# Seven block products in place of eight for 20 of the 32 hidden tiles of the down product

## The chip, the cores and the metric

One core of one Trainium2 chip runs the whole step. The metric is the device time in microseconds; three runs of the kernel before gave 1573.73, 1575.43 and 1575.45, median 1575.43.

## The reference, cut to what matters

One decoder layer for 1024 prompt rows and 8 sample rows (T = 1032 columns; the kernel keeps everything transposed, channels on the 128 partitions). The change touches the second half, with D = 1024 and D_FF = 4096, all in float32:

```python
    x = layer_norm(ALPHA * x + (1 + g1) * m, ln1_g, ln1_b)
    v = x * (1 + sc2) + sh2
    hid = jnp.square(jax.nn.relu(jnp.einsum('bld,df->blf', v, w_up)))
    x = layer_norm(ALPHA * x + (1 + g2) * jnp.einsum('blf,fd->bld', hid, w_down), ln2_g, ln2_b)
```

The gate g2 is one vector for the prompt rows and one for each sample row.

## The kernel before

Every large product is done in three matmuls for one (`term`, L204): a float32 operand is split into a high part (a copy rounded to the faster format fp32r, on ScalarE) and a low part (the rest, a subtraction on VectorE; `split`, L201), and high*high, low*high and high*low are summed in PSUM. `product` (L212) runs, for each of three blocks of 344 columns, all these matmuls into one PSUM bank and then calls an evacuation. A matmul instruction carries a weight load of 128 columns of its own.

The second half has 32 hidden tiles of 128 channels. `hidden(i)` (L949) makes one: 72 matmuls of 344 columns (8 input tiles, 3 terms, 3 blocks), then for each block a relu on ScalarE (from PSUM), a square on VectorE, a rounded copy on ScalarE and a subtraction on VectorE (L944, L945). The down product adds the hidden tiles, times `w_down` and the gate, to the eight residual tiles `x1[m]`, which lie in SBUF in the slabs U0 to U7: `gate_add` (L786) reads a PSUM block on VectorE, multiplies by the gate, adds to `x1[m]` (L789), and treats the 8 sample columns with two small operations (L792, L793).

The tiles are taken in chunks: five of 4 (L985) and two of 6 (L1002). In a chunk of 4, after the four `hidden` come four pairs of output tiles `mp`; each pair takes 2 output tiles, 3 blocks, 4 hidden tiles and 3 terms, which is 72 matmuls of 344 columns, and 6 `gate_add`. In the last chunk the residual is first shifted by a rounded mean (`row_shift`, L994, with the subtractions at L1010) and the second layer norm runs between the last products, over the column blocks of 392, 384 and 256 columns of `LAST`.

Weights come through `weights` (L193), which takes the oldest of two prepared sets and starts on another: a DMA on SP's queue into one of two `raw` buffers (L146), then `parts` splits it into `whi` and `wlo`, two buffers each, so the set after next is split once the set before the next one is used up. The list `order` (L156 to L175) fixes the sequence. PSUM has four banks for `product` (tag mm), one for `ada` and three for `sm`. The order of instructions on each engine is chosen when the kernel is built, by a planner that runs through a time line of its own and, of the instructions that are ready in it, takes the one that stands first in the program; each engine then works through its queue in that fixed order.

Of the kernel before, what the change touches and what calls it, by code (L numbers as in the profile page):

```python
# [17 lines left out]
P = 128  # L18
D = 1024
TP = 1024  # L20
# [34 lines left out]
NFB = 2  # L55
NFA = (DFF // P - 6 * NFB) // 4

# [7 lines left out]
def cols(ap, b):  # L65
    return ap[:, b[0]:b[1]]


def build(tc, ctx, a):
# [10 lines left out]
    pm = ctx.enter_context(tc.tile_pool(name="pm", bufs=MMB, space=PSUM))  # L80
    pq = ctx.enter_context(tc.tile_pool(name="pq", bufs=7 - MMB, space=PSUM))
    dp = ctx.enter_context(tc.tile_pool(name="dp", bufs=1, space=DRAM))

    uid = [0]

    def nm(s):
        uid[0] += 1
        return f"{s}_{uid[0]}"
# [4 lines left out]
    def tmp(w=T, dt=F32):  # L93
        return sp.tile([P, w], dt, tag="t", name=nm("t"), bufs=5)

    def psm():
        return pm.tile([P, 512], F32, tag="mm", name=nm("mm"))
# [69 lines left out]
    for f in range(NFA):  # L167
        order += [("wup", i) + ((("raw", "aw", "yt"),) if i == 2 else ()) for i in range(4 * f, 4 * f + 4)]
        order += [("wda", f, mp) for mp in range(4)]
    spare = [f"U{i}" for i in range(8, 14)] + ["C0", "C1", "C2", "C3", "G", "G"]  # L170
    for f in range(NFB):
        order += [("wup", 4 * NFA + 6 * f + i) for i in range(6)]
        for m in range(8):
            tags = ("raw", spare[2 * m - 4], spare[2 * m - 3])
            order.append(("wdb", f, m) + ((tags,) if f == NFB - 1 and m > 1 else ()))  # L175
# [12 lines left out]
    def prefetch():  # L188
        if order:
            key, raw = load_next()  # L190
            ahead.append((key, parts(*raw)))
# [802 lines left out]
    def row_shift():  # L994

        near, base = tmp(dt=F32R), tmp()
        nc.scalar.copy(near, x1[0])
        for b in BLOCKS:
            ln1.total(base, (cols(near, b),), P, b, w=rones)
        return base  # L1000

    for f in range(NFB):  # L1002
        if f == NFB - 1:
            base = row_shift()
        kh = []
        for i in range(6):
            kh.append(hidden(4 * NFA + 6 * f + i))
            if f == NFB - 1:
                for m in ((0, 1), (2, 3, 4), (5, 6, 7), (), (), ())[i]:
                    tc.keep_in_program_order(tt(x1[m], x1[m], base, op=ALU.subtract))  # L1010
        kf = [(i, h, l) for i, (h, l) in enumerate(kh)]
        if f < NFB - 1:
            for m in range(8):
                product(weights("wdb", f, m), kf, lambda b, ps: gate_add(x1[m], ps, M_G2, m, b))
            continue
# [56 lines left out]
        for m in range(8):  # L1072
            wd.append(weights("wdb", f, m))
            down(m, b)
            if m:
                add_x(m, b)
                add_q(m, b)
# [129 lines left out]
```

## Time and profile before

| | us |
|---|---|
| median of 3 runs | 1575.43 |
| profiled execution, its own time | 1574.45 |
| its span (first to last instruction) | 1572.6 |
| TensorE busy | 1541.8 (98%) |
| VectorE busy | 868.6 (55%) |
| ScalarE busy | 526.3 (33%) |
| mean granted TensorE clock | 0.994 |

A profiled execution is read first by the share of each engine, then by the chain of work that ended last, then by stretches. A matmul's duration in the trace (320 ns at 344 columns) is longer than the distance between two of them, since they overlap; what a matmul costs in a dense stretch is the stretch divided by the count.

### The profile page before, as it was taken

Reading aid. Unit: us, or ns where it says so; the run is one execution under the profiler, and the core shown is the slowest. Engines: PE = TensorE matmul, PEld = TensorE weight load, DVE = VectorE, ACT = ScalarE, POOL = GpSimd, SP = SyncE. Lnnn points to the kernel's source line nnn. Section 1 sums busy time; section 2 is a strip of 40 time slices with the busy share of each in tenths; the row PEclk is TensorE's granted clock in tenths of the full one; section 3 lists DMA queues with packets and bytes.
Section 4 is the critical chain, followed back from the end, with each engine's and each line's share of the span. In section 5 each row is a group of like instructions: output and inputs, shape, how many; then the busy total and the mean of one; then the engine's idle time right before and its main releaser. Section 6 shows DMA issues by size and latency. Waiting matters only on the chain.

```text
span 1572.6 us, 23959 instructions
## 1 busy us (share of the span) xinstructions
PE 1541.8 (98%) x10058; PEld 1489.2 (95%) x10058; DVE 868.6 (55%) x1653; ACT 526.3 (33%) x805; POOL 169.0 (11%) x168
## 2 busy tenths in 40 slices
PE   6999999999999999999999999999999999999996
PEld 5899999999889999999999999999999999999995
DVE  4575556677876742636996444434343433335477
ACT  2553323323333353613577121121312213113334
POOL 0004222221211311100241000000000000000001
PEclk9999999999999999999999999999999999999998
DMA  9332344344343323412221111111111111111102
GB/s 366 114 118 94 108 132 141 118 140 132 135 151 128 119 96 108 175 42 93 82 68 54 41 54 41 48 47 42 53 41 54 41 54 34 45 56 51 61 31 88
DMA packets 49628, 141.44 MB, mean 90 GB/s; under 512 B 5736, under 2 KB 14696, under 8 KB 49520
## 3 DMA queue, kind: packets, MB, share of 16 engines
q1 hardware_dynamic: 49520, 139.91, 27.4%
q8 instruction: 79, 1.29, 0.3%
q14 instruction: 29, 0.24, 0.1%
HBM read 126.33 MB, written 13.56 MB: 89 GB/s over the span
## 4 chain that ended last, share of the span: by engine, by line
PE 94%; DVE 3%; DMA 1%; ACT 1%; issue 1%; POOL 0%; SPq 0%; ACTq 0%; DVEq 0%; POOLq 0%
PE mm L210 86%; PE ada L229 2%; PE sm L651 1%; PE sm L643 1%; PE sm L842 1%; PE sm L638 1%; PE sm L673 1%; PE sm L210 1%; DMA S<-in_xT 0%; PE sm L617 0%; DVE U L1055 0%; PE sm L236 0%; DMA s<-in_ssm 0%; PE sm L597 0%; PE mm L425 0%
## 5 line engine op out<-in xcount | busy, mean ns | idle before, releaser
L210 PE MATMUL mm<-U,whi 128*128 128x344 f32 x3058 | 778.5, 323 | 4.6 <-ACT U L336 4.6
L210 PEld LDWEIGHTS mm<-U,whi 128*128 128x128 f32 x3058 | 536.6, 188 | 21.4 <-issue 11.8
L210 PE MATMUL mm<-U,wlo 128*128 128x344 f32 x1529 | 488.1, 322 | 0.0
L202 ACT CAST whi<-raw 128x1024 fp32r<-128x1024 f32 (+1 forms) x122 | 125.7, 1030 | 544.0 <-PE mm L210 529.8
L210 PEld LDWEIGHTS mm<-U,wlo 128*128 128x128 f32 x1529 | 286.9, 188 | 3.0 <-issue 2.8
L789 DVE SCALAR_TENSOR_TENSOR U<-mm,mod,U 128x344 f32<-128x344 f32 (+3 forms) x216 | 122.7, 571 | 206.5 <-PE mm L210 206.5
L210 PE MATMUL mm<-S,whi 128*128 128x344 f32 (+3 forms) x912 | 232.8, 320 | 0.0
L202 DVE TENSOR_TENSOR wlo<-raw,whi 128x1024 fp32r<-128x1024 f32 (+1 forms) x122 | 146.5, 1201 | 132.2 <-ACT whi L202 131.8
L210 PEld LDWEIGHTS mm<-S,whi 128*128 128x128 f32 x912 | 160.6, 188 | 0.3
L210 PE MATMUL mm<-S,wlo 128*128 128x344 f32 (+3 forms) x456 | 145.3, 320 | 0.0
L210 PE MATMUL mm<-C,whi 128*128 128x344 f32 x516 | 143.0, 320 | 0.0
L944 DVE TENSOR_TENSOR t<-t 128x344 f32<-128x344 f32 x96 | 49.3, 515 | 87.5 <-ACT t L944 87.5
L210 PEld LDWEIGHTS mm<-C,whi 128*128 128x128 f32 x516 | 92.9, 188 | 0.1
L210 PEld LDWEIGHTS mm<-S,wlo 128*128 128x128 f32 x456 | 85.6, 188 | 0.1
L1057 POOL TENSOR_SCALAR U<-U,vec 128x392 f32<-128x392 f32 (+1 forms) x4 | 5.6, 1388 | 720.0 <-DVE U L1055 720.0
L210 PE MATMUL mm<-C,wlo 128*128 128x344 f32 x258 | 82.5, 320 | 0.0
L210 PE MATMUL mm<-G,whi 128*128 128x344 f32 x258 | 82.1, 321 | 0.1
L210 PE MATMUL mm<-xg,whi 128*128 128x344 f32 x258 | 82.0, 320 | 0.0
L387 DVE SCALAR_TENSOR_TENSOR t<-t,vec,t 128x1064 f32<-128x1064 f32 (+1 forms) x52 | 71.8, 1388 | 10.7 <-ACT t L385 9.7
L944 ACT ACTIVATE t<-mm 128x344 f32<-128x344 f32 x96 | 43.6, 455 | 97.0 <-PE mm L210 97.0
L210 PE MATMUL mm<-yc,whi 128*128 128x344 f32 x210 | 66.8, 322 | 0.0
L945 DVE TENSOR_TENSOR S<-t,S 128x344 fp32r<-128x344 f32 x66 | 33.9, 516 | 29.6 <-ACT S L944 29.3
(360 smaller groups left out, 2117.7 us busy)
## 6 DMA issues: line engine op xcount, KB each, us to landing
raw<-in_win SPq DMA_DIRECT2D x44, 512.0 KB, 3.7
aw<-in_wada SPq DMA_DIRECT2D x33, 512.0 KB, 4.2
raw<-in_wup SPq DMA_DIRECT2D x32, 512.0 KB, 3.5
raw<-in_wout SPq DMA_DIRECT2D x24, 512.0 KB, 3.5
raw<-in_wda SPq DMA_DIRECT2D x20, 512.0 KB, 3.5
G<-acd SPq DMA_DIRECT2D x16, 512.0 KB, 3.9
raw<-in_wdb SPq DMA_DIRECT2D x16, 384.0 KB, 3.1
S<-in_xT SPq DMA_DIRECT2D x8, 516.0 KB, 10.2
```

Of the source, the lines that this page charges most:

```text
L202: return nc.scalar.copy(thi, src), tt(tlo, src, thi, op=ALU.subtract)
L210: mm(ps[:, :b[1] - b[0]], wt, cols(xt, b), start=(i == 0 and q == 0), stop=(i == n - 1 and q == 2))
L229: mm(ps[32 * g:32 * g + 32, :256], cs[:, 2 * kp + k2, :], w[:, c:c + 256], start=(kp == 0), stop=(kp == KD // 2 - 1), tile_position=(0, 32 ...
L387: stt(r, t[:, k:k + n], wt(k), r, op0=ALU.mult, op1=ALU.add)
L638: mm(po[:, i * P:(i + 1) * P], st[:, h0:h0 + P], bc[2 + g][:, sl], start=True, stop=True)
L643: mm(py[r * HD:(r + 1) * HD, i * P:(i + 1) * P], xg[g][:, 0, h * HD:(h + 1) * HD], Gs[g][:, h, :], start=True, stop=True, tile_position=(0 ...
L651: mm(pst, bt[:, g * P:(g + 1) * P], xg[g][:, 1], start=True, stop=True)
L673: mm(pn[:, :BW], w, cols(src, b), start=(i == 0), stop=(i == len(srcs) - 1))
L789: stt(dst[:, lo:hi], ps[:, :hi - lo], mod[:, row + m, 0:1], dst[:, lo:hi], op0=ALU.mult, op1=ALU.add)
L842: mm(pn, w, src, start=(i == 0), stop=(i == len(srcs) - 1))
L944: return [lambda: act(x, ps, AF.Relu), lambda: tt(x, x, x, op=ALU.mult), lambda: nc.scalar.copy(xh, x), lambda: tt(xl, x, xh, op=ALU.subtr ...
L945: lambda: tt(xl, x, xh, op=ALU.subtract)]
```

## The change

Hidden tiles 0 to 5 and 26 to 31 keep the plain product, in chunks of 6 at the beginning and the end. The 20 tiles between them form five groups of 4, and in a group each pair of output tiles is done as a 2x2 block product: the 4 hidden tiles are two halves of 2, the 2 output tiles are two halves, and the 1032 columns are two halves of 516. A half of the columns is two runs of 258 (`four`: the first and third quarter, or the second and fourth). Seven products of sums take the place of eight (Winograd's form): `seven` runs them, 12 matmuls of 258 columns each (2 runs, 2 hidden tiles, 3 terms), each into a pair of PSUM banks. Some products are added on top of what a pair holds after it was read; so a pair is read by VectorE (`add_rows`, 516 columns, one operation) and then written on by a later product: `u` takes products 1, 3, 5 and 7, `v` 2 and 6, `y` 4. Seven `add_rows` replace six `gate_add`; the sample columns of three of them are summed in `acc8` and gated at the end.

The operand sums of the hidden tiles (`operands`) and of the weights (`seven_parts`) are made on VectorE and split like the other operands. The split of the four weight sums goes into one single pair of buffers, U2 and U3: for `mp` 0 at once, for 1 and 2 after the `seven` before, and for 3 piece by piece, each sum after the product of `mp` 2 that last reads its place. `hidden_raw` leaves the hidden tile unsplit. Three of the next group's up products stand between the down products (after `operands(0)`, after `mp` 0 and after `mp` 1), the fourth at the head of the next group; `mp` 2 and 3 follow each other directly. U0 and U1 take hidden sums too, and the residual goes to DRAM (`x1d`): each `seven` loads the two rows of the next pair and stores its own two. The PSUM tiles stay single banks as far as the first chunk; `pairs` then closes these pools and opens three pairs for the products and two banks for `sm`. The host lays `w_down` out to suit.

```diff
-NFB = 2
-NFA = (DFF // P - 6 * NFB) // 4
+NFS = 5
+NF = 6
+SPAIR = 0, 2, 1, 3
+QW = T // 4
...
+    stack = ctx.enter_context(ExitStack())
+    pm = stack.enter_context(tc.tile_pool(name="pm", bufs=MMB, space=PSUM))
+    pq = stack.enter_context(tc.tile_pool(name="pq", bufs=7 - MMB, space=PSUM))
...
+    large = []
+    turn = [0]
     def psm():
-        return pm.tile([P, 512], F32, tag="mm", name=nm("mm"))
+        if not large:
+            return pm.tile([P, 512], F32, tag="mm", name=nm("mm"))
+        i = turn[0] % 6
+        turn[0] += 1
+        return large[i % 3][:, i // 3]
+    def pairs():
+        nonlocal pq
+        stack.close()
+        pf = ctx.enter_context(tc.tile_pool(name="pf", bufs=1, space=PSUM))
+        large.extend(pf.tile([P, 2, 512], F32, tag=f"mm{i}", name=f"mm{i}") for i in range(3))
+        pq = ctx.enter_context(tc.tile_pool(name="pg", bufs=2, space=PSUM))
...
-    for f in range(NFA):
-        order += [("wup", i) + ((("raw", "aw", "yt"),) if i == 2 else ()) for i in range(4 * f, 4 * f + 4)]
-        order += [("wda", f, mp) for mp in range(4)]
+    def up(i):
+        return [("wup", i) + ((("raw", "aw", "yt"),) if i == 2 else ())]
+    for i in range(NF):
+        order += up(i)
+    order += [("wdb", 0, m) for m in range(8)]
+    for f in range(NFS):
+        n = NF + 4 * f
+        order += (up(n) if f == 0 else []) + [x for i in SPAIR[f > 0 and 3 or 1:] for x in up(n + i)]
+        nxt = [n + 4 + i for i in (SPAIR if f < NFS - 1 else range(4))]
+        order += up(nxt[0])
+        for mp in range(4):
+            order.append(("wds", f, mp))
+            if mp < 2:
+                order += up(nxt[1 + mp])
+    for i in range(3, NF):
+        order += up(NF + 4 * NFS + i)
     spare = [f"U{i}" for i in range(8, 14)] + ["C0", "C1", "C2", "C3", "G", "G"]
...
+    for m in range(8):
+        tags = ("raw", spare[2 * m - 4], spare[2 * m - 3])
+        order.append(("wdb", 1, m) + ((tags,) if m > 1 else ()))
...
-            ahead.append((key, parts(*raw)))
+            ahead.append((key, parts(*raw) if key[0] != "wds" else seven_parts(raw[0], key[2])))
+    sums2 = []
+    later = []
+    def seven_parts(raw, mp):
+        ha, la = part("whi", F32R, 768), part("wlo", F32R, 768)
+        if not sums2:
+            sums2.extend((part("U2", F32R, 1024), part("U3", F32R, 1024)))
+        hb, lb = sums2
+        a11, a12, a22, a21 = (raw[:, 256 * i:256 * i + 256] for i in range(4))
+        (s1, s2), (s3, s4) = ([t[:, :256], t[:, 256:]] for t in (part("wb", F32, 512), part("wc", F32, 512)))
+        tt(s3, a11, a21, op=ALU.subtract)
+        tt(s1, a21, a22, op=ALU.add)
+        tt(s2, s1, a11, op=ALU.subtract)
+        tt(s4, a12, s2, op=ALU.subtract)
+        got = {}
+        def pieces(src, h, l, *names):
+            w = 256 * len(names)
+            split(src, h[:, :w], l[:, :w])
+            for i, k in enumerate(names):
+                got[k] = h[:, 256 * i:256 * i + 256], l[:, 256 * i:256 * i + 256]
+        pieces(raw[:, :256], ha, la, "a11")
+        pieces(raw[:, 256:768], ha[:, 256:], la[:, 256:], "a12", "a22")
+        def sum_pieces(*names):
+            for k in names:
+                i, src = {"s3": (0, s3), "s2": (1, s2), "s1": (2, s1), "s4": (3, s4)}[k]
+                pieces(src, hb[:, 256 * i:256 * i + 256], lb[:, 256 * i:256 * i + 256], k)
+        if mp:
+            later.append(sum_pieces)
+        else:
+            sum_pieces("s3", "s2", "s1", "s4")
+        return got
...
-    for f in range(NFA):
-        kh = [t[2] for t in two] if f == 0 else []
-        kh += [hidden(4 * f + i) for i in range(len(kh), 4)]
+    eight = cp.tile([P, 8, NS], F32, tag="ysm", name="eight")
+    x1d = [dp.tile([P, T], F32, tag=f"x1d{m}", name=f"x1d{m}") for m in range(8)]
+    kh = [t[2] for t in two] + [hidden(i) for i in range(2, NF)]
+    kf = [(i, h, l) for i, (h, l) in enumerate(kh)]
+    for m in range(8):
+        product(weights("wdb", 0, m), kf, lambda b, ps: gate_add(x1[m], ps, M_G2, m, b))
+        nc.gpsimd.tensor_copy(eight[:, m], x1[m][:, TP:])
+        dma(x1d[m], x1[m])
+    def four(t):
+        return t.rearrange("p (a h c) -> p a h c", a=2, h=2)
+    def hidden_raw(i):
+        r = tmp()
+        product(weights("wup", i), kv, lambda b, ps: act(cols(r, b), ps, AF.Relu))
+        tt(r, r, r, op=ALU.mult)
+        return r
+    sops = {}
+    def operands(j, ra, rb):
+        if j == 0:
+            sops["b11"] = pair(("S0", "S1"))
+        tags = {"b2": (("S2", "S3"), ("U14", "U15")), "odd": (("S4", "S5"), ("yt", "st")), "even": (("S6", "S7"), ("U0", "U1"))}
+        hl = {k: pair(t[j]) for k, t in tags.items()}
+        for k, names in (("b2", ("b21", "b22")), ("odd", ("t1", "t3")), ("even", ("t2", "t4"))):
+            for h, name in enumerate(names):
+                sops[name, j] = [four(t)[:, :, h] for t in hl[k]]
+        for p in range(2):
+            a_, b_ = four(ra)[:, p], four(rb)[:, p]
+            c = (2 * j + p) * QW
+            split(a_[:, 0], *(x[:, c:c + QW] for x in sops["b11"]))
+            t = tmp()
+            t1, t3, t2, t4 = (t[:, i * QW:(i + 1) * QW] for i in range(4))
+            tt(t1, a_[:, 1], a_[:, 0], op=ALU.subtract)
+            tt(t3, b_[:, 1], a_[:, 1], op=ALU.subtract)
+            tt(t2, b_[:, 1], t1, op=ALU.subtract)
+            tt(t4, b_[:, 0], t2, op=ALU.subtract)
+            w = slice(2 * QW * p, 2 * QW * p + 2 * QW)
+            split(rb[:, w], *(x[:, w] for x in hl["b2"]))
+            split(t[:, :2 * QW], *(x[:, w] for x in hl["odd"]))
+            split(t[:, 2 * QW:], *(x[:, w] for x in hl["even"]))
+    acc8 = cp.tile([P, 8, NS], F32, tag="xsm", name="acc8")
+    nc.vector.memset(acc8, 0.0)
+    def add_rows(ps, row, m, h):
+        d = four(row)[:, :, h]
+        if h:
+            tt(acc8[:, m], acc8[:, m], ps[:, 1, QW - NS:QW], op=ALU.add)
+        stt(d, ps[:, :, :QW], mod[:, M_G2 + m, 0:1], d, op0=ALU.mult, op1=ALU.add)
+    def load_rows(mp):
+        rows = [slab(f"U{4 + m % 4}") for m in (2 * mp, 2 * mp + 1)]
+        for i, r in enumerate(rows):
+            dma(r, x1d[2 * mp + i])
+        return rows
+    def seven(f, mp):
+        w = weights("wds", f, mp)
+        m1, m2 = 2 * mp, 2 * mp + 1
+        (r1, r2), last = rows[0], f == NFS - 1
+        if mp < 3 or not last:
+            rows[0] = load_rows((mp + 1) % 4)
+        def multiply(ps, a_, b_, first=False):
+            for p in range(2):
+                for j in range(2):
+                    wh, wl = (t[:, j * P:(j + 1) * P] for t in w[a_])
+                    if b_ == "b11":
+                        xh, xl = (t[:, (2 * j + p) * QW:(2 * j + p + 1) * QW] for t in sops["b11"])
+                    else:
+                        xh, xl = (t[:, p] for t in sops[b_, j])
+                    for q, (wt, xt) in enumerate(((wh, xh), (wl, xh), (wh, xl))):
+                        mm(ps[:, p, :QW], wt, xt, start=first and j == 0 and q == 0, stop=(j == 1 and q == 2),
+                           skip_group_check=not first)
+            if mp == 2 and a_[0] == "s":
+                later[0](a_)
+        u, y, v = (large[(turn[0] + i) % 3] for i in range(3))
+        multiply(u, "a11", "b11", True)
+        add_rows(u, r1, m1, 0)
+        multiply(v, "s3", "t3", True)
+        add_rows(v, r2, m2, 1)
+        multiply(u, "s2", "t2")
+        add_rows(u, r2, m2, 0)
+        multiply(y, "a12", "b21", True)
+        add_rows(y, r1, m1, 0)
+        multiply(u, "s1", "t1")
+        add_rows(u, r2, m2, 1)
+        multiply(v, "a22", "t4")
+        add_rows(v, r2, m2, 0)
+        multiply(u, "s4", "b22")
+        add_rows(u, r1, m1, 1)
+        if last and mp > 1:
+            x1[m1], x1[m2] = r1, r2
+        else:
+            for m, r in ((m1, r1), (m2, r2)):
+                dma(x1d[m], r)
+    pairs()
+    rows = [load_rows(0)]
+    r = [hidden_raw(NF + i) for i in SPAIR]
+    for f in range(NFS):
+        n = NF + 4 * f
+        nxt = [n + 4 + i for i in (SPAIR if f < NFS - 1 else range(4))]
+        if f:
+            r.append(hidden_raw(n + SPAIR[3]))
+        operands(0, r[0], r[1])
+        more = [hidden_raw(nxt[0])]
+        operands(1, r[2], r[3])
         for mp in range(4):
-            w = weights("wda", f, mp)
-            for m in (2 * mp, 2 * mp + 1):
-                product(w, [(4 * (m % 2) + i, h, l) for i, (h, l) in enumerate(kh)],
-                        lambda b, ps: gate_add(x1[m], ps, M_G2, m, b))
...
+            seven(f, mp)
+            if mp < 3:
+                done = later.pop(0)
+                if mp < 2:
+                    done("s3", "s2", "s1", "s4")
+            turn[0] += 1
+            if mp < 2:
+                more.append(hidden_raw(nxt[1 + mp]))
+        r = more
+    kh = []
+    for x in r:
+        h, l = pair(ht[hn % len(ht)])
+        hn += 1
+        split(x, h, l)
+        kh.append((h, l))
+    for m in range(4):
+        x1[m] = slab(f"U{m}")
+        dma(x1[m], x1d[m])
+    tt(acc8, acc8, mod[:, M_G2:M_G2 + 8, 1:9], op=ALU.mult)
+    tt(acc8, acc8, eight, op=ALU.add)
+    for m in range(8):
+        nc.gpsimd.tensor_copy(x1[m][:, TP:], acc8[:, m])
+    for i in range(3, NF):
+        kh.append(hidden(NF + 4 * NFS + i))
+        if i == 3:
+            near, base = tmp(dt=F32R), tmp()
+            nc.scalar.copy(near, x1[0])
+            for b in BLOCKS:
+                ln1.total(base, (cols(near, b),), P, b, w=rones)
+        for m in ((0, 1, 2, 3), (4, 5, 6, 7), ())[i - 3]:
+            tc.keep_in_program_order(tt(x1[m], x1[m], base, op=ALU.subtract))
+    kf = [(i, h, l) for i, (h, l) in enumerate(kh)]
+    if ks:
         total = ln1.total
...
```

## Rows read from the trace of the kernel before

**Rows 1.** Page, part 1 (busy time, share, instructions) and part 4 (chain by engine).
```profile
PE 1541.8 (98%) x10058; PEld 1489.2 (95%) x10058; DVE 868.6 (55%) x1653; ACT 526.3 (33%) x805; POOL 169.0 (11%) x168
...
PE 94%; DVE 3%; DMA 1%; ACT 1%; issue 1%; POOL 0%; SPq 0%; ACTq 0%; DVEq 0%; POOLq 0%
```

**Rows 2.** Chain of waits in order of time, from 842 us: start, length, what.
```profile
842.18 572.69 PE mm L210 x3630
...
1415.34 99.09 PE mm L210 x606
```

**Rows 3.** Stretches: busy time and count by engine, clock, DMA share, GB/s.
```profile
842.18:1414.55 572.37, 572.37 (x3630) 572.37 (x3630) 231.34 (x449) 129.37 (x220) 0.00 (x0) 1.00 0.15 47
1483.31:1508.84 25.53, 25.53 (x146) 25.53 (x144) 19.02 (x42) 9.48 (x15) 0.00 (x0) 1.00 0.24 78
1535.58:1540.10 4.52, 4.52 (x40) 4.52 (x39) 4.32 (x9) 1.37 (x3) 0.33 (x1) 1.00 0.12 44
```

**Rows 4.** VectorE groups by shape, from 842 us: busy us, mean ns | idle.
```profile
L202 DVE TENSOR_TENSOR wlo<-raw,whi 128x1024 fp32r<-128x1024 f32 x49 | 60.0, 1225 | 77.0 <-ACT whi L202 77.0
L789 DVE SCALAR_TENSOR_TENSOR U<-mm,mod,U 128x344 f32<-128x344 f32 x96 | 55.2, 575 | 93.4 <-PE mm L210 93.4
L944 DVE TENSOR_TENSOR t<-t 128x344 f32<-128x344 f32 x95 | 48.8, 515 | 86.8 <-ACT t L944 86.8
...
L789 DVE SCALAR_TENSOR_TENSOR U<-mm,mod,U 128x384 f32<-128x384 f32 x16 | 9.8, 614 | 6.4 <-PE mm L210 6.4
...
L1010 DVE TENSOR_TENSOR U<-U,t 128x1032 f32<-128x1032 f32 x8 | 9.4, 1227 | 0.0
...
L792 DVE TENSOR_TENSOR gs<-mm,mod 128x8 f32<-128x8 f32 x56 | 8.7, 156 | 0.0
...
L789 DVE SCALAR_TENSOR_TENSOR U<-mm,mod,U 128x256 f32<-128x256 f32 x8 | 3.8, 479 | 0.0
...
L1040 DVE TENSOR_TENSOR xg<-yc,xg 128x256 f32<-128x256 f32 x1 | 0.4, 425 | 0.8 <-ACT yc L846 0.8
```

**Rows 5.** Timeline of VectorE, 874 to 885 us: start, length, what [idle].
```profile
877.34 1.05 DVE L789 SCALAR_TENSOR_TENSOR U<-mm,mod,U 128x344 f32<-128x344 f32 x2 [3.06 <-PE mm L210]
...
882.39 1.22 DVE L202 TENSOR_TENSOR wlo<-raw,whi 128x1024 fp32r<-128x1024 f32 x1 [0.28 <-ACT whi L202]
883.54 0.57 DVE L789 SCALAR_TENSOR_TENSOR U<-mm,mod,U 128x344 f32<-128x344 f32 x1
```

**Rows 6.** ScalarE groups by shape, the same stretch and columns.
```profile
L202 ACT CAST whi<-raw 128x1024 fp32r<-128x1024 f32 x49 | 51.4, 1049 | 267.6 <-PE mm L210 267.6
L944 ACT ACTIVATE t<-mm 128x344 f32<-128x344 f32 x94 | 42.7, 455 | 97.0 <-PE mm L210 97.0
L944 ACT CAST S<-t 128x344 fp32r<-128x344 f32 x64 | 30.6, 481 | 50.5 <-DVE t L944 50.5
```

**Rows 7.** Timeline of all engines at a block's end, 879 us.
```profile
879.03 0.47 PE L210 MATMUL mm<-S,whi 128*128 128x344 f32 x2
...
879.38 0.58 DVE L789 SCALAR_TENSOR_TENSOR U<-mm,mod,U 128x344 f32<-128x344 f32 x1 [0.72 <-PE mm L210]
```

**Rows 8.** Timeline of all engines, 734 to 736 us: TensorE waits for VectorE.
```profile
734.11 1.22 DVE L202 TENSOR_TENSOR S<-raw,S 128x1024 fp32r<-128x1024 f32 x1
...
734.50 0.32 PE L210 MATMUL mm<-U,whi 128*128 128x344 f32 x1
...
735.38 0.59 PE L210 MATMUL mm<-yc,S 128*128 128x344 f32 x2 [0.56 <-DVE S L202]
```

**Rows 9.** DMA issues of the whole run: count, KB each, us to landing.
```profile
raw<-in_wda SPq DMA_DIRECT2D x20, 512.0 KB, 3.5
...
ycd<-yc SPq DMA_DIRECT2D x8, 516.0 KB, 3.1
t<-ycd SPq DMA_DIRECT2D x8, 516.0 KB, 4.6
U<-in_xT SPq DMA_DIRECT2D x8, 516.0 KB, 7.9
```

More of the change, by code (lines that the diff above doesn't have):

```diff
@@ L79, in build @@
     sp = ctx.enter_context(tc.tile_pool(name="sp", bufs=1))
-    pm = ctx.enter_context(tc.tile_pool(name="pm", bufs=MMB, space=PSUM))
-    pq = ctx.enter_context(tc.tile_pool(name="pq", bufs=7 - MMB, space=PSUM))
     dp = ctx.enter_context(tc.tile_pool(name="dp", bufs=1, space=DRAM))
+    stack = ctx.enter_context(ExitStack())
+    pm = stack.enter_context(tc.tile_pool(name="pm", bufs=MMB, space=PSUM))
+    pq = stack.enter_context(tc.tile_pool(name="pq", bufs=7 - MMB, space=PSUM))
     uid = [0]
@@ L166, in build @@
             order.append(("wout", 1, m) + ((("raw", f"S{m}", f"S{m + 1}"),) if m % 2 == 0 else ()))
-    for f in range(NFA):
-        order += [("wup", i) + ((("raw", "aw", "yt"),) if i == 2 else ()) for i in range(4 * f, 4 * f + 4)]
-        order += [("wda", f, mp) for mp in range(4)]
-    spare = [f"U{i}" for i in range(8, 14)] + ["C0", "C1", "C2", "C3", "G", "G"]
[L171 to L175, printed above, removed]
+    def up(i):
[14 more added lines that the diff above has]
+        order += up(NF + 4 * NFS + i)
+    spare = [f"U{i}" for i in range(8, 14)] + ["C0", "C1", "C2", "C3", "G", "G"]
+    for m in range(8):
+        tags = ("raw", spare[2 * m - 4], spare[2 * m - 3])
+        order.append(("wdb", 1, m) + ((tags,) if m > 1 else ()))
     ahead = []
@@ L983, in build @@
         after(rescale(k, b), vcopy)
-    for f in range(NFA):
-        kh = [t[2] for t in two] if f == 0 else []
-        kh += [hidden(4 * f + i) for i in range(len(kh), 4)]
-        for mp in range(4):
-            w = weights("wda", f, mp)
-            for m in (2 * mp, 2 * mp + 1):
-                product(w, [(4 * (m % 2) + i, h, l) for i, (h, l) in enumerate(kh)],
-                        lambda b, ps: gate_add(x1[m], ps, M_G2, m, b))
[L994 to L1015, printed above, removed]
+    eight = cp.tile([P, 8, NS], F32, tag="ysm", name="eight")
@@ L1072, in build @@
         for m in range(8):
-            wd.append(weights("wdb", f, m))
+            wd.append(weights("wdb", 1, m))
             down(m, b)
@@ L1165 @@
     a["wup"] = c_(g["w_up"][0].reshape(KD, P, 32, P).transpose(2, 1, 0, 3)).reshape(32, P, 1024)
-    wd, cut = g["w_down"][0], 4 * NFA * P
-    a["wda"] = c_(wd[:cut].reshape(NFA, 4, P, 4, 2, P).transpose(0, 3, 2, 4, 1, 5)).reshape(NFA, 4, P, 1024)
-    a["wdb"] = c_(wd[cut:].reshape(NFB, 6, P, 8, P).transpose(0, 3, 2, 1, 4)).reshape(NFB, 8, P, 768)
+    wd = g["w_down"][0].reshape(32, P, 8, P)
+    ends = np.stack([wd[:NF], wd[32 - NF:]])
+    a["wdb"] = c_(ends.transpose(0, 3, 2, 1, 4)).reshape(2, 8, P, NF * P)
+    mid = wd[NF:32 - NF].reshape(NFS, 2, 2, P, 4, 2, P)
+    mid = np.stack([mid[:, h, :, :, :, m] for h, m in ((0, 0), (1, 0), (1, 1), (0, 1))])
+    a["wds"] = c_(mid.transpose(1, 4, 3, 0, 2, 5)).reshape(NFS, 4, P, 1024)
     a["vec"] = c_(np.concatenate(
```

## Prediction

> **What bounds the kernel now.** I read the page first: TensorE is busy 98% of the span and holds 94% of the chain that ended last, VectorE 55% and 3% [rows 1]. Then the chain in order of time: from 842.18 us it is one piece of matmuls, 572.69 us long, and after three matmuls of the row shift another of 99.09 us [rows 2]. So from the first up product to the last chunk nothing that another engine does is seen in the end; only fewer or cheaper matmuls, or a new wait, can move it. Then the stretches, for what a matmul costs at each width, at a granted clock of 1.00: 572.37 us for 3630 of 344 columns is 157.7 ns each; 25.53 us for 144 of 392 (143 steps) is 178.5; 4.52 us for 39 of 256 (38 steps) is 118.9 [rows 3]. The last two give 0.438 ns per column, and on that line 344 columns would take 157.4, which is the first row. So the price is nearly proportional to the columns, with about 7 ns fixed. VectorE is busy 231.34 of the 572.37 us there, 40%, and ScalarE 129.37, 23% [rows 3].
>
> **What is removed and added on TensorE.** Per pair of output tiles, 72 matmuls of 344 columns go: 72 x 157.7 = 11,354 ns. 84 of 258 columns come: 118.9 + 2 x 0.438 = 119.8 ns each, 10,063 ns. That is 1.29 us less, and there are 5 x 4 = 20 such pairs: 25.8 us less. No other matmul changes in number: 32 up products, 12 hidden tiles in plain down products. It would take 135.2 ns per matmul of 258 columns for the gain to vanish (11,354 / 84).
>
> A rule speaks against just this. The Trainium skill, "TensorE: Matmul & The Clock Gate", section "Back-to-back issue gap", gives for a stream of weight loads and matmuls about 81 ns at 128 columns and 131 at 512, so that much of the price would not depend on the columns. Between its figures I estimate 97.9 ns at 258 and 109.1 at 344, 84 x 97.9 - 72 x 109.1 = +0.37 us per pair, 7 us slower in all. The rows differ in level and slope: the measurement decides.
>
> **What comes on VectorE.** One read of a pair of banks (516 columns from PSUM) is not in the trace; 256, 344 and 384 columns take 479, 575 and 614 ns [rows 4], 1.05 ns per column, so 0.755 us. From below: two block reads in a row start 1.05 - 0.58 = 0.47 us apart [rows 5], so at least 0.65; from above, two separate reads of 256 take 0.96. I take 0.755, nearest to the row of 384. A subtraction in SBUF of 256 columns takes 425 ns; 344 and 1032 columns take 515 and 1227 [rows 4], so 512 take 0.69.
> - Per `seven`: 7 reads 5.3 us, 3 small sums 0.5, 4 weight sums 1.7, the low parts (256, 512, four times 256) 2.8: 10.3 us, beside 10.06 us of TensorE.
> - Per group, `operands`: 4 runs, each five operations of 258 columns and three of 516, 4.2 us: 17 us.
> - Per up product: a square of 1032 columns and one weight subtraction, 1.23 + 1.23 = 2.5 us, beside 72 x 157.7 = 11.35 us.
>
> A group is 4 x 10.06 + 4 x 11.35 = 85.7 us on TensorE and 41 + 17 + 10 = 68 us on VectorE, 79% in place of 40%. Operations in a row overlap by about 0.1 us [rows 5]; with 120 operations it is nearer 57 us, 66%. So VectorE still fits, but not in every stretch: in a `seven` 20 operations, 10.3 - 1.8 = 8.5 of 10.06 us, and with the square and the weight split that belong to a neighbouring up product some 10 of 10. ScalarE: a cast of 256 columns is 0.41 us by the casts of 344 and 1024 (0.481 and 1.049 [rows 6]); per `seven` 2.7, per group of operands 9, per up product 3 x 0.455 + 1.05 = 2.4, together 29 of 85.7 us: it hides.
>
> **The new wait.** Product 5 writes on the pair that VectorE reads after product 3, product 7 on the one read after 5, product 2 of the next pair of tiles on the one read after 7: one product, 12 x 119.8 = 1.44 us, lies between. Behind a waiting matmul stands all of TensorE. The read starts 0.20 us after the next product's first matmul (879.38 against the second matmul of the first line, 879.19 [rows 7]), takes 0.755, and the matmul starts 0.05 us after VectorE's end (735.33 to 735.38 [rows 8]): 1.0 of 1.44 us. After products 5 and 7 the small sum goes first (0.156 [rows 4]): 1.2. So alone it is hidden, with 0.25 to 0.45 us to spare. What stands in front decides: a read that became free during a weight subtraction started right at its end, 883.54, 1.15 us after that began [rows 5]. The Trainium skill, "PSUM — Partial Sum Buffer", section "Engine vs sequencer instructions", says that VectorE's queue is strictly first in, first out; the row agrees, and with a queue that let the read pass none of the following losses would be there (a time near 1549).
>
> A subtraction of 425 ns in front costs nothing or up to 0.2 us; one of 1.2 us up to 0.9. Each `seven` has one or two of these long ones in its time (the neighbour's square, its weight split), and three of seven turnarounds are short, so I take 0.3 us per `seven`, 6 us (bounds: 0, where they fall on `v` and `y`, and 1.3 us per `seven`, 26 us, where each short turnaround is late by 0.4).
>
> **The operands of a group.** Between one group's last `seven` and the next one's first lie two up products, 22.7 us, with 17 us of `operands`, two squares, two weight splits and the next weights' 4.5 us on VectorE: 26 us by durations, some 22 by starts. The last operand is first needed by product 3, 3 us into `seven`, so I take 0.4 us per group, 2 us (from 0 to 3 us per group, where the queue before has not been worked off). Groups start with all tiles made long ago except one.
>
> **Transfers.** Each `seven` adds two loads and two stores of 516 KB. Such rows took 4.6 us (load), 3.1 (store) and 7.9 where many came at once [rows 9]. On SP's queue the stores wait for the last read, and the next weights (512 KB, 3.5 us) stand behind them; those are used an up product later, 11.35 us. The tightest is `mp` 3: its rows are loaded while `mp` 2 runs (10.06 us), into slabs whose stores went out an up product before. Hidden; without the cover it would be up to 8 us in a group. DMA was busy 15% of this stretch [rows 3]; a group adds 16 x 516 KB, 8.5 MB in 85 us, 100 GB/s on 47.
>
> **The ends.** `pairs` waits for the last evacuation of the plain chunk: at most a read with its small ones, 1 us, once. After the last group, four rows come back from DRAM (8 us) and eight small copies are made while the up product of 11.35 us runs; the row shift comes behind it, one wait on ScalarE's copy of 1032 columns (1.05 us) or none: 0.5 us. In the last chunk six banks stand for four and two `sm` banks for three; the final stage's chain runs over VectorE already, so 0 (from -1 to +2).
>
> **The sum**, against the profiled execution's own 1574.45 us (span 1572.6): -25.8 + 6 + 2 + 1 + 0.5 = -16.3, so 1558.1. The median of the runs shown, 1575.43, lies 1 us above that execution, so a median may be 1559; the losses were taken in the middle of wide bounds, and fewer collisions are likelier than more, as several of these operations fall under up products, where nothing waits. I predict 1558.
>
> **Rivals.**
> 1. *VectorE becomes the bound in the stretch of two `seven` in a row and the operands behind it.* For: 10 of 10 us there. Against: each group also has two up products with 11.35 us each and hardly 6 us of VectorE, which take up a backlog. If short turnarounds are late by 0.3 us each, 1 us per `seven`: 20 us, and 1 us per group: 1574.45 - 25.8 + 20 + 5 + 1.5 = 1575; half of that, 1563. This case covers 1566 to 1575. Chance 0.18.
> 2. *Slower: the weight pieces stand in front of the reads in the fixed order.* A piece becomes free with the same product as the read, and by program it comes first; then the read waits for ScalarE's cast and the subtraction: 0.2 + 0.41 + 0.05 + 0.425 + 0.755 + 0.05 = 1.9 us against 1.44, 0.45 us at each of three turnarounds, 0.6 with the small sum. With `mp` 2 alone, 5 x 1.6 = 8 us, not enough; if the operand pieces, squares and weight splits queue in the same way in all 20, 20 x 1.6 = 32 and the groups' 3 us, 15: 1574.45 - 25.8 + 32 + 15 + 1.5 = 1597. It decides from 1.3 us lost per `seven`. For: ready at the same moment, a weight cast ahead of the relu is what ScalarE's long waits on TensorE look like (267.6 us of idle before the cast, ended by L210 [rows 6]). Against: a piece's subtraction is not ready with the read, its cast has to run first. Chance 0.12.
> 3. *The price of a matmul does not fall with the columns* (258 columns in two runs, pairs of banks, sums on top of what is there). At the old 157.7 it would be 84 x 157.7 - 11,354 = +1.89 us, 38 us slower: 1612. Against: 256 columns in the same kernel at 118.9 [rows 3]. Chance 0.03.
> 4. *The forecast*, losses of 0 to 0.8 us per `seven`: 1549 to 1566. Chance 0.67.
>
> **Range and chances.** The range goes from the sum without any loss, 1548 (1574.45 - 25.8), to 1571, which takes in more than half of rival 1; about 0.18 is left out. Faster by over 0.2% (3 us, what a measurement tells from no change) is the forecast and most of rival 1: 0.83; within 0.2%: 0.04; slower: 0.13.
>
> **What would show it.** Right: the stretch of the groups has matmuls of 258 columns about 120 ns apart inside a product; gaps ahead of products 2, 5 and 7, each ended by the read of 516 columns, together under 10 us; VectorE near 70% busy there; the read at 0.7 to 0.8 us. Wrong: a distance over 130 ns inside products; gaps of over 1 us in most `seven`; TensorE waiting for DMA rows or for the operands' subtractions.

## The result and the profile after

The changed kernel took 1557.88 us (median of four runs, 1557.47 to 1558.65) beside 1575.44 for the kernel before in the same comparison (1573.73 to 1575.52): ratio 0.9896, 95% interval 0.9883 to 0.9908. The forecast was 1558.0 in a range of 1548 to 1571. The profiled execution took 1557.72, 16.7 less than the one of before; its span is 1555.7.

The page answers to [rows 1]: TensorE still fills the span, VectorE rises from 55 to 63%.

```profile
PE 1522.9 (98%) x10298; PEld 1464.8 (94%) x10298; DVE 976.5 (63%) x1884; ACT 566.2 (36%) x919; POOL 173.6 (11%) x184
...
PE 93%; DVE 4%; issue 1%; ACT 1%; DMA 1%; SPq 0%; ACTq 0%; DVEq 0%
```

Three stretches, with the columns of [rows 3]: the five groups, one dense run of 258 columns, and the 392 columns of the last chunk.

```profile
1018.57:1436.40 417.83, 415.06 (x3002) 410.56 (x3001) 274.75 (x554) 127.91 (x258) 0.00 (x0) 1.00 0.44 140
1062.90:1077.97 15.07, 15.07 (x128) 15.07 (x126) 12.40 (x24) 5.31 (x12) 0.00 (x0) 1.00 0.39 128
1467.16:1492.74 25.58, 25.58 (x146) 25.58 (x144) 19.06 (x42) 9.47 (x15) 0.00 (x0) 1.00 0.25 78
```

In the second, 126 matmuls fill 15.07 us from the first start to the last one's, 125 steps of 120.6 ns. VectorE is busy 274.75 of 417.83 us in the groups, 66%, ScalarE 31%. The last chunk costs what it did. VectorE's groups by shape in the same stretch, columns as in [rows 4]:

```profile
L1109 DVE SCALAR_TENSOR_TENSOR U<-mm,mod,U 128x516 f32<-128x516 f32 x139 | 103.9, 749 | 15.4 <-PE mm L1133 11.7 <-DMA U<-x1d 3.0
...
L1108 DVE TENSOR_TENSOR acc<-acc,mm 128x8 f32<-128x8 f32 x59 | 9.1, 155 | 58.7 <-PE mm L1133 58.7
```

A read of a pair of banks takes 749 ns, and ahead of the reads VectorE is idle for over 70 us: mostly it waits for TensorE, not the reverse. TensorE's waits from 829 to 1467 us (who <- whom: us, times, longest):

```profile
PE mm L1133 <- DVE U L1109: 1.7, 10, 0.2
PE mm L278 <- DVE gs L860: 0.8, 1, 0.8
```

1.7 us is too little. A matmul's drawn duration (0.28 us) is more than twice its cadence (0.12), so the drawing covers part of a wait. By the distances from start to start there are 19 places in the groups where a product's first matmul comes 0.17 to 0.36 us late and its second about 0.1 more; each starts 0.05 to 0.15 us after the end of a read. There are four per group, three in the last, 7.7 us in all: 15 ahead of product 7, four ahead of product 6, none ahead of products 2 and 5. Two words for what follows: a turnaround runs from a product on a pair to the next product on the same pair, with the read in between; its cover is the time of the other matmuls that stand in it. The first kind of wait, twice per group, on TensorE (start, length):

```profile
1115.30 0.28 PE L1133 MATMUL mm<-S,whi 128*128 128x258 f32 x1
...
1117.44 0.28 PE L1133 MATMUL mm<-st,U 128*128 128x258 f32 x1
1117.56 0.28 PE L1133 MATMUL mm<-S,wlo 128*128 128x258 f32 x1
...
1118.04 0.28 PE L1133 MATMUL mm<-U,whi 128*128 128x258 f32 x1
1118.16 0.32 PE L278 MATMUL mm<-U,whi 128*128 128x344 f32 x1
1118.64 0.63 PE L1133 MATMUL mm<-S,U 128*128 128x258 f32 x3 [0.17 <-DVE U L1109]
```

and the same moment on VectorE:

```profile
1117.76 0.16 DVE L1108 TENSOR_TENSOR acc<-acc,mm 128x8 f32<-128x8 f32 x1 [4.81 <-PE mm L1133]
1117.84 0.75 DVE L1109 SCALAR_TENSOR_TENSOR U<-mm,mod,U 128x516 f32<-128x516 f32 x1
```

The first line on TensorE is the first matmul of product 6, the second the last one of product 5. VectorE had been idle for 4.81 us and began 0.20 us after the next matmul's start, as [rows 7] have it; nothing stood in front. But between product 5 and product 7 on the same pair lie only five matmuls of product 6 and one of an up product, 5 x 0.12 + 0.16 = 0.76 us of cover, against 0.28 + 0.75 + 0.05 = 1.08 from the first of them to the first matmul that the read lets go. With the second matmul's delay 0.43 us is lost; in the first group, where one turnaround has two up matmuls (0.92 us of cover), 0.28. TensorE's queue does not follow the program: the planner put the first seven matmuls of product 6 ahead of product 5. The third wait of a group is of the same kind, in pair `mp` 3: five up matmuls (0.79 us) between products 2 and 6, which share a pair. In the fourth, there too, product 7 waits for the read after 5, which on VectorE stands behind the read after 2 (both add to the same row) and three more operations:

```profile
1170.27 0.75 DVE L1109 SCALAR_TENSOR_TENSOR U<-mm,mod,U 128x516 f32<-128x516 f32 x1
1170.94 0.15 DVE L1108 TENSOR_TENSOR acc<-acc,mm 128x8 f32<-128x8 f32 x1
1171.01 0.42 DVE L270 TENSOR_TENSOR U<-wc,U 128x256 fp32r<-128x256 f32 x1
1171.34 0.42 DVE L1091 TENSOR_TENSOR t<-t 128x258 f32<-128x258 f32 x1
1171.68 0.42 DVE L1092 TENSOR_TENSOR t<-t,t 128x258 f32<-128x258 f32 x1
1172.02 0.75 DVE L1109 SCALAR_TENSOR_TENSOR U<-mm,mod,U 128x516 f32<-128x516 f32 x1
```

`pairs`, at the change from single banks, costs one wait; TensorE's queue there:

```profile
961.72 0.39 PE L278 MATMUL mm<-yc,whi 128*128 128x344 f32 x1 [0.83 <-DVE gs L860]
```

So the profiles' difference is accounted for: columns 20 x (72 x 157.7 - 84 x 120.4 ns) = -24.8 us (120.4 is the mean between the 120.6 above and the 120.3 over all products); late turnarounds +7.7; `pairs` +1.07 from start to start; from the first matmul of 392 columns to the span's end 88.54 in place of 89.29, -0.75. Sum -16.8, measured -16.7. Part of this agreement is chance: the place where the two kernels part comes 0.41 us later in this execution (829.28 and 829.69 us), so the stretch from there to the last chunk is some 0.5 us shorter than its three terms make it.

### The profile page after: what moved, and what is told of

The parts are those of the page before. It is cut to its first block, busy times and chain, and to the rows that moved or that the text cites. A ratio compares the mean times of both kernels' runs of the same rounds, so it can differ in the third digit from the quotient of the medians.

```text
span 1555.7 us, 25048 instructions
## 1 busy us (share of the span) xinstructions
PE 1522.9 (98%) x10298; PEld 1464.8 (94%) x10298; DVE 976.5 (63%) x1884; ACT 566.2 (36%) x919; POOL 173.6 (11%) x184
## 4 chain that ended last, share of the span: by engine, by line
PE 93%; DVE 4%; issue 1%; ACT 1%; DMA 1%; SPq 0%; ACTq 0%; DVEq 0%
PE mm L278 72%; PE mm L1133 13%; PE ada L297 2%; PE sm L719 1%; PE sm L711 1%; PE sm L910 1%; DVE U L1109 1%; PE sm L706 1%; PE sm L741 1%; PE sm L278 1%; DMA raw<-in_win 1%; PE sm L685 0%; DVE U L1248 0%; PE sm L304 0%; DMA s<-in_ssm 0%
## 5 line engine op out<-in xcount | busy, mean ns | idle before, releaser
L278 PE MATMUL mm<-U,whi 128*128 128x344 f32 x2914 | 733.7, 324 | 3.7 <-ACT U L404 3.7
L270 ACT CAST whi<-raw 128x1024 fp32r<-128x1024 f32 (+2 forms) x142 | 123.3, 882 | 367.3 <-PE mm L278 350.0
L270 DVE TENSOR_TENSOR wlo<-raw,whi 128x1024 fp32r<-128x1024 f32 (+2 forms) x142 | 143.5, 1014 | 126.3 <-ACT whi L270 125.4
L1109 DVE SCALAR_TENSOR_TENSOR U<-mm,mod,U 128x516 f32<-128x516 f32 x140 | 104.7, 749 | 15.4 <-PE mm L1133 11.7
L857 DVE SCALAR_TENSOR_TENSOR U<-mm,mod,U 128x344 f32<-128x344 f32 (+3 forms) x96 | 54.5, 569 | 90.6 <-PE mm L278 90.6
L1133 PE MATMUL mm<-S,U 128*128 128x258 f32 x480 | 85.4, 286 | 2.2 <-DVE U L1109 1.7
L1133 PE MATMUL mm<-S,whi 128*128 128x258 f32 x320 | 73.6, 284 | 0.5
L1133 PEld LDWEIGHTS mm<-S,U 128*128 128x128 f32 x480 | 68.8, 189 | 5.6 <-DVE U L1109 4.0
L278 PE MATMUL mm<-S,whi 128*128 128x344 f32 (+3 forms) x240 | 61.2, 320 | 0.0
L1133 PEld LDWEIGHTS mm<-S,whi 128*128 128x128 f32 x320 | 55.6, 189 | 1.7 <-DVE U L1109 1.7
```

What stands on the lines that cost most here:

```text
L270: return nc.scalar.copy(thi, src), tt(tlo, src, thi, op=ALU.subtract)
L278: mm(ps[:, :b[1] - b[0]], wt, cols(xt, b), start=(i == 0 and q == 0), stop=(i == n - 1 and q == 2))
L857: stt(dst[:, lo:hi], ps[:, :hi - lo], mod[:, row + m, 0:1], dst[:, lo:hi], op0=ALU.mult, op1=ALU.add)
L1109: stt(d, ps[:, :, :QW], mod[:, M_G2 + m, 0:1], d, op0=ALU.mult, op1=ALU.add)
L1133: mm(ps[:, p, :QW], wt, xt, start=first and j == 0 and q == 0, stop=(j == 1 and q == 2), skip_group_check=not first)
```

## Experiments

All times are medians beside the kernel before on the same chip, ratios to that with 95% intervals; the changed kernel itself stands at 0.9896. The kernel before stood at 1574.43 to 1575.59 in these comparisons, so a difference of about 1 us to the changed kernel's 1557.88 says nothing. In the expectations theory A says that the order chosen for TensorE's queue spends the cover of the turnarounds; theory B, the forecast's reason, that the reads themselves come late on VectorE; other rivals that rows or weight sums are what waits.

**Program order on TensorE.**

```diff
+    with tc.manual_schedule(engines={mybir.EngineType.PE}):
         for f in range(NFS):      # the groups, indented
```

> The five groups with TensorE kept in the order of the program: the seven products of a pair one behind the other, each up product whole. Theory A (cover spent early: the changed kernel's 19 waits of 0.4 us on a read of 516 columns, 7.7 us in all, stand where the planned order has moved the other product or the block of an up product that would lie in the turnaround to an earlier place): one product of 1.44 us lies in each turnaround, which needs 1.0 to 1.2 us, so most waits go, and the time falls from 1557.9 to 1551 to 1554. Theory B (the reads stand behind other operations in VectorE's queue): with no blocks of up products in the turnarounds the waits grow, above all in the third and fourth pair, to 10 to 20 us: 1560 to 1570.

1561.7 us, 0.9916 [0.9903, 0.993]: theory A's number is missed, theory B's met. Waits on TensorE, 844 to 1470 us:

```profile
PE mm L1133 <- DVE U L1109: 2.5, 4, 1.6
PE mm L1133 <- ACT S L270: 1.6, 4, 0.4
```

From start to start it is some 12 us: reads up to 1.75 late, operand casts, and relus that product 2 waits for, which the planned order had put other work around. With one whole product in each turnaround reads do come late on VectorE. The latest of them, however, is not the forecast's case of a read behind a long operation: it stands behind two weight sums, and VectorE is idle because the first of them waits for its weights:

```profile
1255.99 0.42 DVE L234 TENSOR_TENSOR wc<-raw 128x256 f32<-128x256 f32 x1 [1.63 <-DMA raw<-in_wds]
1256.34 0.42 DVE L235 TENSOR_TENSOR wb<-raw 128x256 f32<-128x256 f32 x1
1256.67 0.75 DVE L1109 SCALAR_TENSOR_TENSOR U<-mm,mod,U 128x516 f32<-128x516 f32 x1
```

Program order takes away some waits and brings others.

**No turnaround at all**: the seven products take the three pairs in rotation and always start afresh, so nothing is added on top of a pair just read.

```diff
...
+        for k, (a_, b_, r_, m_, h_) in enumerate(steps):
+            multiply(ps[k % 3], a_, b_, True)
+            add_rows(ps[k % 3], r_, m_, h_)
```

> Leaves out the adding of products 3, 5, 6 and 7 on top of what a pair holds: all seven start fresh, on the three pairs in turn, so two products (2.9 us) lie in each turnaround; the output changes, the work of every engine does not. If the 7.7 us of waits come from the turnaround of pairs (theories A and B): 1550 to 1552. If they come from rows, weights or operand sums that are late: 1556 to 1558, with the waits still there.

1550.51, 0.9848 [0.9835, 0.9862], 7.4 us below the changed kernel. In the groups one wait is left:

```profile
PE mm L278 <- DVE gs L860: 0.8, 1, 0.8
PE mm L1133 <- DVE U L1109: 0.8, 1, 0.8
```

The first row is `pairs`; the read of the second stands, as in the run above, behind a weight sum that waits for its weights. The 7.4 us are the size of the 19 waits. The turnaround is the cause: the work of VectorE and the DMA queues is the same here. Whether its cover was short or its read late this run does not tell, since two products would hide both.

**An eighth product**, to price twelve matmuls and the cover they give.

```diff
         multiply(y, "a12", "b21", True)
+        multiply(y, "a12", "b21")
```

> Doubles one product of each pair of output tiles (12 more matmuls of 258 columns on pair y, 240 in all; the output changes). If what a matmul costs is its distance of 120.4 ns and TensorE sets the end: 28.9 us more, less the waits that the added product covers (0 to 7 us): 1580 to 1587. If VectorE sets the pace in the groups, the added products lie in its shadow: under 1572.

1579.0, 1.0027 [1.0017, 1.0037], 21.1 us above the changed kernel and 1 under the expected range, which let at most 7 us of waits go: 240 x 120.4 ns are 28.9; no wait on a read is left in the groups, which gives 7.7 back: 21.2. With eight products the columns are those of before (96 x 258 = 72 x 344), and so, within 0.4%, is the time: the gain of the change is the product left out.

**No round trip of rows**: the stores of a `seven` are left out and its rows loaded once only.

```diff
+        if mp % 2 not in held:
...
-            for m, r in ((m1, r1), (m2, r2)):
-                dma(x1d[m], r)
```

> Leaves out the loads and stores of the residual rows between the groups (two pairs of rows are loaded once and added to; the output changes). If the transfers are hidden, as forecast: 1557 to 1559, the same waits on reads. If rows or the weights behind the stores on SP's queue hold the reads: 1550 to 1555.

1558.32, 0.9896 [0.9882, 0.9909], with the same 19 waits. The 516 KB transfers (stores 3.3 us, loads 4.6 from issue to landing in the changed kernel) are hidden.

**Weight sums split as a whole** for `mp` 3 too, not piece by piece.

```diff
-            if mp == 2 and a_[0] == "s":
-                later[0](a_)
...
-                done = later.pop(0)
-                if mp < 2:
-                    done("s3", "s2", "s1", "s4")
+                later.pop(0)("s3", "s2", "s1", "s4")
```

> The weight sums of the fourth pair are split together after the third pair's seven products, as for the second and third pair, and not piece by piece. In the third pair four casts and subtractions of 256 columns go from VectorE's queue among the reads and come to stand between the third and the fourth pair. If pieces ahead of the reads cost (rival 2 of the prediction): the same or faster, 1553 to 1558. If the pieces are what keeps the fourth pair fed: the four sums (4 x 0.42 us, behind casts of 0.41) are late for its second and third product, 0.5 to 2 us per group: 1560 to 1568.

1557.74, 0.9892 [0.9877, 0.9907]: no difference, and the same 19 waits. Rival 2 of the prediction, weight pieces in front of reads, costs nothing that can be measured.

**No operand and weight sums**: eight sums of 258 columns per `operands` call and four of 256 per weight set are left out, and the products run on unsummed parts. VectorE is relieved of 13.5 us per group.

```diff
-        tt(s3, a11, a21, op=ALU.subtract)
...
+        s1, s2, s3, s4 = a21, a22, a12, a11
...
```

> Leaves out the additions and subtractions that make the block sums, of weights (4 of 256 columns per pair) and of hidden tiles (16 of 258 per group); unsummed tiles are split in their place, the output changes. VectorE loses 13.5 of some 55 us per group. If the waits are cover spent early (theory A): they stay, 1555 to 1558. If they are VectorE's queue (theory B): they go, 1550 to 1552.

1559.94, 0.9905 [0.9892, 0.9919]: not faster, and above both ranges. Waits, 843 to 1468 us:

```profile
PE mm L1123 <- DVE U L1099: 2.1, 10, 0.3
PE mm L274 <- ACT whi L266: 1.9, 4, 0.5
```

From start to start the waits on reads come to 6.0 us in 15 places, in place of 7.7 in 19. They follow the cover and not VectorE's load. Half of the first kind now have two up matmuls and lose 0.28 us, the others lose 0.43 as before, with VectorE idle ahead of both. The third kind is gone, with eight up matmuls in its place. The fourth, whose read stands behind other work, loses up to 0.5. The second row is a side effect (a weight cast that comes late on ScalarE; why was not followed up), 3.5 us from start to start.

**The products alone in order**, up products free to move: an order on TensorE's queue (no data wait) puts each product behind the one before it.

```diff
-                        mm(ps[:, p, :QW], wt, xt, ...)
+                        ins = mm(ps[:, p, :QW], wt, xt, ...)
+                        if p == 0 and j == 0 and q == 0 and b_ in KEEP and prev:
+                            after(ins, prev[-1])
+            prev.append(ins)
```

Here KEEP names products 2 to 7.

> Holds each of the seven products of a pair behind the one before it in the program, by an order on TensorE's queue alone; blocks of up products may still stand between. In the planned queue product 4 then stands before 5, product 6 between 5 and 7, and a product of the next pair before the last one. Theory A: the 16 to 19 waits of 0.43 us go, as in the rotating pairs: 1550 to 1553. Theory B: as with TensorE in program order, waits behind VectorE's queue: 1556 to 1562.

1572.81, 0.9987 [0.9978, 0.9995]: most of the gain is lost, and both theories' numbers are missed. Once per group the planner now puts the first product of `mp` 3 ahead of product 7 of `mp` 2, so that product 2 of `mp` 3 follows directly on the pair that 7 has just filled. TensorE, then VectorE at that place:

```profile
1079.44 0.75 PE L1135 MATMUL mm<-S,U 128*128 128x258 f32 x3 [2.38 <-DVE U L1109]
```

```profile
1076.46 0.75 DVE L1109 SCALAR_TENSOR_TENSOR U<-mm,mod,U 128x516 f32<-128x516 f32 x1
1077.13 1.43 DVE L270 TENSOR_TENSOR S<-t,S 128x258 fp32r<-128x258 f32 x4
1078.47 0.16 DVE L1108 TENSOR_TENSOR acc<-acc,mm 128x8 f32<-128x8 f32 x1
1078.55 0.75 DVE L1109 SCALAR_TENSOR_TENSOR U<-mm,mod,U 128x516 f32<-128x516 f32 x1
```

A turnaround without cover, and its read behind another read and four low parts. The wait is not the whole price; the stretch behind it, and one behind another wait of this kind (columns of [rows 3]):

```profile
1079.44:1083.00 3.56, 3.56 (x18) 3.56 (x19) 2.55 (x8) 0.41 (x1) 0.00 (x0) 0.54 0.73 283
...
1261.57:1265.13 3.56, 3.55 (x29) 3.56 (x30) 2.83 (x9) 0.76 (x2) 0.00 (x0) 1.00 0.79 315
```

For 3.56 us after the wait the granted clock was 0.54, near the lower of its two levels (1.2 of 2.4 GHz), and matmuls of 258 columns stood 214 ns apart. The clock fell after three of the five waits of this kind (2.33 to 2.54 us from start to start); after the other two (the last row is behind one of them) it stayed at 1.00. In this trace, which is of the slowest of eleven executions (1575.64), the late starts in the groups come to 23.0 us: 12.5 in the five waits, 4.4 at the lower clock, and 6.1 in shorter waits.

**Product 4 alone held behind 3** (the same edit with KEEP `b21`).

> Holds back only product 4 (pair y) until product 3 is issued; all else is free. In the planned queue it then covers the turnaround from product 3 and the matmuls of an up product cover the one from 5 to 7. Theory A: 1550 to 1553, the waits under 1.5 us in all. Theory B: 1556 to 1562.

1567.58, 0.9953 [0.9941, 0.9966]: both theories' numbers are missed. Waits, 844 to 1476 us:

```profile
PE mm L1135 <- ACT t L1070: 7.7, 11, 0.8
PE mm L1135 <- DVE U L1109: 1.5, 5, 0.3
...
PE mm L1135 <- DVE U L270: 0.7, 4, 0.2
```

Product 2 starts on a pair that the last block of an up product has just filled, and ScalarE's relu has to read it first; at 1043 us, the longest of these waits, the relu stands behind a weight cast of 1.05 us. In the changed kernel product 4 stood between them; its early place was worth more there than as cover later.

**The pairs of `v` and `y` exchanged**, so that product 4, not 2, takes the pair that the up product used last.

```diff
-        u, y, v = (large[(turn[0] + i) % 3] for i in range(3))
+        u, v, y = (large[(turn[0] + i) % 3] for i in range(3))
```

> Exchanges the PSUM pairs of v and y and nothing else. In the changed kernel v takes the pair that the last block of an up product, or product 7 of the pair of tiles before, has just used, and product 2 writes on it one product later; now product 2 takes the pair that was free longest and y (product 4) the late one, so one turnaround in four is gone. The planned order of TensorE also changes: no product 4 in second place. Theory C (the waits are the sum of turnarounds that the planned order leaves without cover, and the assignment of pairs sets which): 1550 to 1555, no waits on the relu. Theory B (VectorE's queue is late whatever the pairs are): 1556 or more.

1550.54, 0.9841 [0.9828, 0.9855], as theory C expected. The groups show no wait on a read, and their late starts come to 0.8 us in all. One line gives back the 7 us.

**Exchanged, and the products in order** (KEEP 2 to 7), and **exchanged, and TensorE in program order**.

> The exchange of v and y together with the seven products of a pair held in order (the run e7_products_in_order had a wait of 2.4 us per group, of product 2 of the fourth pair on the read of product 7 of the third, and relus at 0.3 us). Theory C: both kinds are gone with the exchange: 1550 to 1553. Theory B: VectorE's backlog at the third and fourth pair shows elsewhere, over 1558.

> The exchange with all of TensorE in program order in the groups (e1_pe_in_program_order waited 12 us: relus 3 x 0.3, a cast of an operand 0.55 and reads of 0.3 to 1.7 us per group). Theory C: the relus' and part of the reads' waits go, 1553 to 1557. Theory B: 1559 or more.

1560.75, 0.9906 [0.9892, 0.9919], and 1559.96, 0.9904 [0.989, 0.9918]: theory C's numbers are missed, theory B's met, twice. In the first, TensorE's waits from 844 to 1469 us:

```profile
PE mm L1135 <- DVE U L1109: 5.4, 14, 1.1
```

and one of them on VectorE:

```profile
1130.06 1.22 DVE L270 TENSOR_TENSOR wlo<-raw,whi 128x1024 fp32r<-128x1024 f32 x1 [6.83 <-ACT whi L270]
1131.20 0.75 DVE L1109 SCALAR_TENSOR_TENSOR U<-mm,mod,U 128x516 f32<-128x516 f32 x1
```

The read starts when a weight subtraction of 1.22 us ends: just the collision that the forecast described, in another order than the one it was forecast for. The longest waits of both kernels, 0.9 to 1.3 us, once in each of four groups, are those of the program order again: the read stands behind weight sums that wait for their weights.

**Product 6 alone held behind 5** (KEEP `t4`, pairs as in the change).

> The changed kernel with its own pairs; only product 6 is held behind product 5. In the planned queue of the first and second pair product 6 then lies whole between 5 and 7, where the changed kernel has one matmul of an up product; product 4 stays in second place. Theory A: the waits of product 7 in the first and second pair (10 of 0.43 us) go: 1553 to 1555. Theory B (one product is not cover enough, since the read of product 5 stands behind other operations of VectorE): they stay at 0.3 us or more each: 1556 or more.

1548.93 (1547.95 to 1549.48), 0.9835 [0.9822, 0.9849]: the fastest median, though its interval overlaps that of the exchange, and faster than theory A expected, for the waits of the fourth pair are gone as well. Products 5, 6 and 7 are whole and follow each other, except in `mp` 3, where product 2 and a block of 24 up matmuls stand between 5 and 6. TensorE and VectorE in a place that answers to 1117 us above (TensorE from the last matmul of product 5):

```profile
1114.16 0.28 PE L1135 MATMUL mm<-st,U 128*128 128x258 f32 x1
1114.28 0.28 PE L1135 MATMUL mm<-S,whi 128*128 128x258 f32 x1
...
1115.58 0.28 PE L1135 MATMUL mm<-U,whi 128*128 128x258 f32 x1
1115.71 0.52 PE L1135 MATMUL mm<-S,U 128*128 128x258 f32 x3
```

```profile
1114.56 0.75 DVE L1109 SCALAR_TENSOR_TENSOR U<-mm,mod,U 128x516 f32<-128x516 f32 x1
1115.23 0.42 DVE L270 TENSOR_TENSOR U<-wb,U 128x256 fp32r<-128x256 f32 x1
```

From product 6's first matmul to product 7's there are 1.43 us; the read ends 1.03 after the former (1114.56 + 0.75 - 1114.28). No wait on a read is left from 842 to 1460 us, nor a start in the groups that is over 0.06 us late. The first matmul of 392 columns starts at 1458.44 in place of 1467.16, 8.7 earlier, 1.1 of it from before the groups: 7.6, the 7.7 above.

## Why the prediction was right, and where it was not

- *What bounds the kernel*: right. TensorE is at 98%, and every change between these kernels is a matmul or a wait on TensorE.
- *Columns*: -25.8 forecast, -24.8 measured: 120.4 ns for 119.8. The Trainium skill, "TensorE: Matmul & The Clock Gate", section "Back-to-back issue gap", was weighed with an estimate of 97.9 ns at 258 columns and +7 us for the change; the trace does not agree, and rival 3 falls with it.
- *The read of a pair*: 0.755 forecast, 749 ns measured, with its start and release as in [rows 7, 8]. VectorE at 66% as forecast by starts; rival 1 does not occur.
- *The new wait*: 6 us forecast, and 2 for the operands; 7.7 measured, all in turnarounds. **The step that failed is its reason**, and that the sum came out is luck. The prediction put one whole product, 1.44 us, into each turnaround, as the program has it, and let long operations in front of the read make 0.3 us per `seven`. But TensorE's queue had been reordered: two of four late turnarounds in a group had 0.76 us of cover and one 0.79, against about 1.08 needed, with the read starting at once. Only the fourth has a read behind other work, and not behind a long operation. The evidence: with no turnaround (1550.51), and with the full product back in it (1548.93), the waits are gone, while relieving VectorE (1559.94) leaves 6.0 us of them, less only where the cover is longer. The 0.25 to 0.45 us that the prediction saw to spare with a whole product is what the held product 6 shows (1.43 us of cover against 1.08). Product 6, ahead of which four waits stand, the prediction did not count among the short turnarounds at all. The sum came out because two terms with the wrong reason had the right size together, inside bounds as wide as 0 to 26 us.
- *The operands of a group*: 2 us forecast, none seen; in the changed kernel no TensorE wait in the groups is ended by an operand.
- *Rival 2*, weight pieces: one subtraction of 0.42 us stands among the three of the fourth kind, and splitting the sums as a whole changes nothing.
- *Transfers* hidden: right for the changed kernel. The margin is small: with TensorE in program order a read stood behind a weight sum that waited for its weights, and TensorE with it, up to 1.75 us. *`pairs`*: 1 forecast, 1.07. *Ends*: +0.5 forecast, -0.75.

My first cure fell too. "Restore the program's order" was theory A's advice, and its five forms cost 2 to 15 us over the changed kernel, for the order was also hiding relus, casts and busy reads. What holds is narrower: this order left one product's cover too short, and moving that product (or the pairs) is enough. Why the planner began product 6 before 5 was not examined. That the exchange and the held product act in the same way is read from their traces only in so far as both have no such wait left.

## What to carry to other kernels

When an accumulator is read and written on again, take the cover from the order in which the engine's queue really runs, not from the program, and hold it against the whole turnaround (here 1.08 us for 516 columns). Look for late starts by distances from start to start, as drawn durations showed 1.7 of 7.7 us here. Try single orders on the chip, one at a time: the same kind of edit gave 9 us (7.6 of them in the groups, by the traces), or took 15.

## What was not expected of the hardware

With the products in order TensorE waited five times for about 2.4 us. After three of these waits the granted clock fell: to 0.54 over the 3.56 us behind the first, with a matmul of 258 columns at 214 ns in place of 120. After the other two, of the same length, it stayed at 1.00, as it did after the waits of 0.4 us in the changed kernel. So a long wait can cost more than its length, here in three cases of five; what made the difference the runs do not show.
